# A two-layer encoder in split float32: the feed-forward part in four chunks of 3, 3, 3 and 2 column groups instead of three of 4, 4 and 3

## The chip, the cores and the metric

The kernel runs on one core of one Trainium2 chip. The metric is the device time of one execution in microseconds (us). Before the change the median of three runs is 2045.35 us (2045.31 to 2046.12). 0.2% of that is 4.1 us.

## The reference

Two layers over 256 tokens of width 2048. Each layer has a token mixer (layer 0 gates within 128-token chunks, layer 1 is grouped-query attention) and a cross-attention into 256 memory tokens, which share one input and one output projection, and then a feed-forward network (FFN) of inner width 5632. All inputs are float32. What matters here:

```python
def swiglu(h, w_gate_up, w_down):
    gate, up = jnp.split(h @ w_gate_up, 2, axis=-1)      # h: 256 x 2048, w_gate_up: 2048 x 11264
    return (jax.nn.silu(gate) * up) @ w_down             # w_down: 5632 x 2048

for l in range(2):
    ...
    x = x + jnp.concatenate([tok_out, mem_out], axis=-1) @ w_out[l]
    x = x + swiglu(rms_norm(x, g_ffn[l]), w_gate_up[l], w_down[l])
```

## The kernel before

**Split products.** Every float32 operand is split into a high half (rounded to float32r) and a low half (the rest). ScalarE makes the high half of weights (L254, `whi`), VectorE the low half (L255, `wlo`: the raw weights less `whi`). One product of 128 x 128 activations with 128 x 512 weights is three matmuls (`matmul3`, L198 to L200): high by high, low activations by high weights, high activations by low weights.

**Column groups and chunks.** The FFN has 11 column groups `f`, each 512 columns of gate and the same 512 of up. A chunk is a run of groups: first gate_up is computed for every group of the chunk, then the part of w_down that takes the chunk's features is added to the residual tiles `X`. Before the change the chunks are groups 0 to 3, 4 to 7 and 8 to 10.

**Pairs.** The class `Pair` does two 128-token rows (t = 0, 1) times two 512-column blocks at once. Its unit `i` is a pair of 128-feature rows, 2 x 2 blocks of weights: 1 MB, fetched by two DMAs into one of four `raw` tiles. A unit is done in one of two ways. `eight` does the plain eight products, 24 matmuls. `seven` does seven products in Strassen's manner, 21 matmuls; it needs four additions on the weights (L347 to L350, in `prepare`: one in place, three into a tile `T` of which there are two), one more pair of halves (of the 128 x 1536 `T`), and sums of the activations (`activation_sums`: four 128 x 128 subtractions, L303 to L306, and a split). At the end of its last `seven` unit a Pair folds the PSUM banks 1, 5, 6 and 7 together on VectorE (`inner`, L397 to L401) and adds the results into the output (L405); at the end of each half (t) of its last unit it adds the banks 2, 3, 4 and 8 (`outer`, L413). Banks 1, 5, 6 and 7 come from one ring of four PSUM tiles (`m`, which the transposes use as well), banks 2, 3, 4 and 8 from another (`acc`).

**Rings that pace the weights.** `raw` has 4 tiles, `whi` and `wlo` 3 each. A `seven` unit takes two of `whi` and two of `wlo` (raw and T), an `eight` one of each.

**A chunk's stages.** gate_up of one group is a Pair of 8 units, three of them `seven` (two in group 0). After it, ScalarE and VectorE make silu(gate) x up (L785, L786), and `turn_a` transposes the result on TensorE (L204), splits it (L192, L193) and, for units in `quick`, makes the activation sums. w_down of a chunk is two Pairs one after the other (`jj` = 0, 1, each 1024 output columns), each over all feature pairs of the chunk, two per group. `quick` names the feature pairs that are done as `seven`: in a chunk of four, two of eight; in the last chunk of three, none in layer 0 and one in layer 1. In w_down the order of a four-group Pair is, counted within the chunk, 0, 2, 1, 4, 3, 5, 6, 7 for `jj` = 0 and 1, 0, 3, 2, 4, 5, 6, 7 for `jj` = 1, with 1 and 3 as `seven`.

**What sets the order.** Small steps (`turn_a`, the additions of `inner`, the norms of the next layer) are put off by a count of ticks (`later`); each Pair unit ticks twice. The last group of a chunk is turned at the third and fourth tick of w_down, the other groups at the 12th and 13th tick of the next gate_up. The order in which the program is written is a priority: at build, a planner lays each engine's instructions into one fixed list by its own estimate of when each could run, so a list can hold the high-half products of a later unit ahead of the low-half products of an earlier one. On the chip each list runs in that order.

**The end of each layer's FFN.** In the last chunk of layer 0 each finished pair of `X` blocks starts the norm of layer 1 (`residual_turns`); in that of layer 1 the blocks are stored to the output.

Of the kernel before, what the change touches and what calls it, by code (L numbers as in the profile page):

```python
# [53 lines left out]
def encoder(ctx: ExitStack, tc: tile.TileContext, x, mem, g_mix, g_ffn, w_in_a, g_v_a, w_spatial, b_spatial,  # L54
# [16 lines left out]
    def nm(s):  # L71
        uid[0] += 1
        return f"{s}_{uid[0]}"

    def big(dt=F32, shape=None):
        return room["p"].tile(shape or [P, NB], dt, tag="a", name=nm("a"))
# [4 lines left out]
    def misc():  # L81
        return psm.tile([P, NB], F32, tag="m", name=nm("m"))

    def v4(a):
        return a.rearrange("p (c n) -> p c n", n=P)
# [10 lines left out]
    def later(delay, fn):  # L96
        queue.append((clock[0] + delay, len(queue), fn))
# [39 lines left out]
    def gslice(kind, l):  # L137
        return gcol[kind][:, 16 * l:16 * l + 16]
# [49 lines left out]
    def split(src, shape):  # L188

        hi = big(F32R, shape)  # L190
        lo = big(F32R, shape)
        nc.scalar.copy(hi, src)  # L192
        nc.vector.tensor_tensor(lo, src, hi.bitcast(F32), ALU.subtract)  # L193
        return hi, lo
# [7 lines left out]
    def transpose4(src, dst):  # L202
        for c in range(4):
            nc.tensor.transpose(dst[:, c * P:(c + 1) * P], src[:, c * P:(c + 1) * P], ident)  # L204
# [95 lines left out]
    def activation_sums(a0, a1):  # L300

        q = big(F32, [P, 4, P])
        nc.vector.tensor_tensor(q[:, 0], a1[:, 0], a1[:, 1], ALU.subtract)  # L303
        nc.vector.tensor_tensor(q[:, 2], a1[:, 0], a0[:, 0], ALU.subtract)
        nc.vector.tensor_tensor(q[:, 1], a0[:, 0], q[:, 0], ALU.subtract)
        nc.vector.tensor_tensor(q[:, 3], a0[:, 1], q[:, 1], ALU.subtract)  # L306
        hi, lo = split(q, [P, 4, P])
        return [(hi[:, i, :], lo[:, i, :]) for i in range(4)]
# [290 lines left out]
    def residual_turns(j, norm, g, parts):  # L599
        add_residual(None, j, norm, g, parts)  # L600
# [4 lines left out]
    for l in range(DEPTH):  # L605
# [151 lines left out]

        hT = Parts()
        next_norm = Norm()
        for chunk in (range(0, 4), range(4, 8), range(8, 11)):  # L760
            aT, aS, half = Parts(), {}, {}
            quick = [2 * f + 1 for f in chunk[:2 if chunk[-1] < 10 else l]]

            def turn_a(a, t, f, aT=aT, aS=aS, half=half, quick=quick):
                tp = misc()
                transpose4(a, tp)
                hi, lo = split(v4(tp), [P, 4, P])
                for i in range(4):
                    aT.put(4 * f + i, t, hi[:, i, :], lo[:, i, :])
                i = 2 * f + 1  # L770
                if i in quick:
                    half[i, t] = big(F32, [P, 2, P])
                    nc.scalar.copy(half[i, t], v4(tp)[:, 2:4])
                    if t == NT - 1:
                        aS[i] = activation_sums(half[i, 0], half[i, 1])

            pairs = {}
            for f in chunk:
                order, some = ((3, 4, 5, 0, 6, 1, 7, 2), 2) if f == 0 else ((0, 3, 1, 4, 2, 5, 6, 7), 3)
                pairs[f] = Pair(hF, sums, w_gate_up[l], f * NB, DFF + f * NB, order, fast[:some])  # L780
            for f, g in pairs.items():
                g.run(pairs.get(f + 1))
                for t in range(NT):
                    a = kp.tile([P, NB], F32, tag="sg", name=nm("sg"), bufs=2)
                    nc.scalar.activation(a, g.out[t][0], AF.Silu, scale=norm.r[t])  # L785
                    nc.vector.scalar_tensor_tensor(a, g.out[t][1], norm.r[t], a, ALU.mult, ALU.mult)  # L786
                    later(3 + t if f == chunk[-1] else 12 + t, lambda a=a, t=t, f=f: turn_a(a, t, f))
            last = chunk[-1] == 10
            every = [2 * f + c for f in chunk for c in range(2)]
            slow = [i for i in every if i not in quick]  # L790
            pairs = []
            for jj in range(2):
                order = list(slow)
                for n, i in enumerate(quick):
                    order.insert(2 * n + (0 if jj and not last else 2), i)
                into = [[X[t][2 * jj + n] for n in range(2)] for t in range(NT)]
                pairs.append(Pair(aT, aS, w_down[l], 2 * jj * NB, (2 * jj + 1) * NB, order, quick, into))
            for jj, g in enumerate(pairs):
                g.run(None if jj else pairs[1])
                for j in (2 * jj, 2 * jj + 1):  # L800
                    if last and l < DEPTH - 1:
                        residual_turns(j, next_norm, gslice("mix", l + 1), hT)
                    elif last:
                        for t in range(NT):
                            parts = 2 if j == 3 and t == NT - 1 else 1
                            for i in range(parts):
                                cs = slice(i * NB // parts, (i + 1) * NB // parts)
                                eng = nc.scalar if i else nc.sync
                                eng.dma_start(out[0, t * P:(t + 1) * P, j * NB + cs.start:j * NB + cs.stop],
                                              X[t][j][:, cs])  # L810
# [37 lines left out]
```

## Time and profile before

| | |
|---|---|
| median of 3 runs | 2045.35 us |
| profiled execution, whole | 2045.77 us |
| its span, first to last instruction | 2044.0 us |
| TensorE (PE) busy | 2028.7 us, 99% |
| VectorE (DVE) busy | 1604.7 us, 79% |
| ScalarE (ACT) busy | 1095.1 us, 54% |
| weights and others moved by DMA | 396.08 MB, 194 GB/s in the mean |

The busy times of PE are unions of instructions whose ends are modelled; how fast it really goes is read from the distance between the starts of matmuls. A busy time of VectorE counts its instructions once where two overlap. The FFN of layer 0 runs from about 340 to 1030 us of the span, that of layer 1 from about 1355 us to the end.

### The profile page before, as it was taken

What the parts mean: (1) busy time and instruction counts of PE and PEld (TensorE: products, weight loads), DVE (VectorE), ACT (ScalarE), POOL (GpSimd) and SP (SyncE); (2) the same over time, 40 slices, a digit from 0 to 9 for tenths busy, and PEclk for the clock granted to TensorE, in tenths of its full rate; (3) what the DMA queues carried; (4) which work ended last, traced back from release to release, by engine and by line L of the source; (5) the groups of instructions that cost most, each with busy time, mean ns of one, the idle gap of its engine ahead of it and who ended that gap; (6) DMA issues with size and microseconds to landing.
All of it is one profiled execution on the core that took longest, in us unless ns stands there. A gap on an engine that the chain in (4) does not pass through costs nothing.

```text
span 2044.0 us, 24691 instructions
## 1 busy us (share of the span) xinstructions
PE 2028.7 (99%) x9298; PEld 1679.5 (82%) x9298; DVE 1604.7 (79%) x1862; ACT 1095.1 (54%) x1389; POOL 49.1 (2%) x80
## 2 busy tenths in 40 slices
PE   8999999999999999999999999999999999999999
PEld 6888888888888888888888888888888888888887
DVE  5575557998888988887666876589979899798976
ACT  7765455455444554445556665555544455444552
POOL 2010000000000000000010100000000000000000
PEclk9999999999999999999999999999999999999999
DMA  9754554655656556566556434655666555665554
GB/s 330 249 177 159 187 187 148 227 168 203 208 190 220 169 201 208 200 215 209 188 190 212 157 124 142 206 179 172 205 206 211 200 176 195 206 216 196 181 197 138
DMA packets 202432, 396.08 MB, mean 194 GB/s; under 512 B 11068, under 2 KB 11432, under 8 KB 202312
## 3 DMA queue, kind: packets, MB, share of 16 engines
q1 hardware_dynamic: 198800, 385.79, 56.4%
q0 software_dynamic: 2048, 6.42, 1.0%
q10 hardware_dynamic: 1464, 2.28, 0.3%
q8 instruction: 73, 1.20, 0.2%
q14 instruction: 47, 0.39, 0.1%
HBM read 390.26 MB, written 4.19 MB: 193 GB/s over the span
## 4 chain that ended last, share of the span: by engine, by line
PE 94%; DVE 3%; DMA 1%; issue 1%; ACT 1%; SPq 0%; DVEq 0%; ACTq 0%
PE acc L200 27%; PE acc L198 27%; PE acc L199 27%; PE m L200 4%; PE m L198 4%; PE m L199 4%; PE m L204 2%; DVE wlo L255 1%; DMA raw<-in_w_gate_up 1%; ACT whi L254 0%; PE m L500 0%; DMA x<-in_x 0%; DMA raw<-in_w_down 0%; PE m L643 0%; DVE x L413 0%
## 5 line engine op out<-in xcount | busy, mean ns | idle before, releaser
L255 DVE TENSOR_TENSOR wlo<-raw,whi 128x2048 fp32r<-128x2048 f32 (+2 forms) x465 | 836.4, 1822 | 227.0 <-ACT whi L254 224.8
L254 ACT CAST whi<-raw 128x2048 fp32r<-128x2048 f32 (+2 forms) x465 | 700.9, 1539 | 584.6 <-PE acc L199 513.3
L198 PE MATMUL acc<-whi,h 128*128 128x512 f32 x1440 | 563.6, 392 | 0.8 <-ACT whi L254 0.8
L199 PE MATMUL acc<-whi,h 128*128 128x512 f32 x1440 | 562.6, 391 | 0.0
L200 PE MATMUL acc<-wlo,h 128*128 128x512 f32 x1440 | 523.8, 392 | 1.1 <-DVE wlo L255 1.1
L198 PE MATMUL acc<-whi,a 128*128 128x512 f32 x1062 | 415.4, 392 | 0.6 <-DVE a L431 0.6
L199 PE MATMUL acc<-whi,a 128*128 128x512 f32 x1062 | 414.9, 391 | 0.0
L200 PE MATMUL acc<-wlo,a 128*128 128x512 f32 x1062 | 398.8, 391 | 0.1
L200 PEld LDWEIGHTS acc<-wlo,h 128*128 128x128 f32 x1440 | 270.6, 188 | 56.9 <-DVE wlo L255 1.9
L198 PEld LDWEIGHTS acc<-whi,h 128*128 128x128 f32 x1440 | 270.7, 188 | 55.4 <-ACT whi L254 1.2
L199 PEld LDWEIGHTS acc<-whi,h 128*128 128x128 f32 x1440 | 270.6, 188 | 55.0
L200 PEld LDWEIGHTS acc<-wlo,a 128*128 128x128 f32 x1062 | 199.7, 188 | 41.5 <-DVE wlo L255 0.5
L198 PEld LDWEIGHTS acc<-whi,a 128*128 128x128 f32 x1062 | 199.9, 188 | 41.3 <-DVE a L431 0.8
L199 PEld LDWEIGHTS acc<-whi,a 128*128 128x128 f32 x1062 | 199.9, 188 | 40.5
L254 ACT CAST whi<-T 128x1536 fp32r<-128x1536 f32 x82 | 121.4, 1481 | 143.3 <-PE acc L199 104.1
L255 DVE TENSOR_TENSOR wlo<-T,whi 128x1536 fp32r<-128x1536 f32 x82 | 143.5, 1750 | 38.8 <-ACT whi L254 38.8
L198 PE MATMUL m<-whi,a 128*128 128x512 f32 x264 | 104.2, 395 | 0.7 <-ACT whi L254 0.7
L199 PE MATMUL m<-whi,a 128*128 128x512 f32 x264 | 102.8, 390 | 0.0
L347 DVE TENSOR_TENSOR raw<-raw 128x512 f32<-128x512 f32 x82 | 56.1, 684 | 56.4 <-DMA raw<-in_w_gate_up 54.3
L200 PE MATMUL m<-wlo,a 128*128 128x512 f32 x264 | 89.6, 389 | 0.0
L192 ACT CAST a<-m 128x512 fp32r<-128x512 f32 x80 | 46.3, 586 | 50.7 <-PE m L204 32.6
L193 DVE TENSOR_TENSOR a<-m,a 128x512 fp32r<-128x512 f32 x80 | 54.0, 683 | 17.5 <-ACT a L192 17.5
(126 smaller groups left out, 1469.0 us busy)
## 6 DMA issues: line engine op xcount, KB each, us to landing
raw<-in_w_gate_up SPq DMA_DIRECT2D x352, 512.0 KB, 4.7
raw<-in_w_down SPq DMA_DIRECT2D x176, 512.0 KB, 5.2
raw<-in_w_out SPq DMA_DIRECT2D x32, 1024.0 KB, 5.1
raw<-in_w_in_a SPq DMA_DIRECT2D x24, 1024.0 KB, 5.3
raw<-in_w_in_b SPq DMA_DIRECT2D x24, 1024.0 KB, 5.2
raw<-in_w_mem_kv SPq DMA_DIRECT2D x16, 1024.0 KB, 5.2
raw<-in_w_in_a SPq DMA_DIRECT2D x7, 512.0 KB, 6.1
x<-in_x SPq DMA_DIRECT2D x8, 256.0 KB, 5.7
```

The lines of the kernel that those rows point to most:

```text
L192: nc.scalar.copy(hi, src)
L193: nc.vector.tensor_tensor(lo, src, hi.bitcast(F32), ALU.subtract)
L198: nc.tensor.matmul(out, lhsT=a[0], rhs=b[0], start=start, stop=False)
L199: nc.tensor.matmul(out, lhsT=a[1], rhs=b[0], start=False, stop=False)
L200: nc.tensor.matmul(out, lhsT=a[0], rhs=b[1], start=False, stop=stop)
L204: nc.tensor.transpose(dst[:, c * P:(c + 1) * P], src[:, c * P:(c + 1) * P], ident)
L254: nc.scalar.copy(hi[:, cut], raw[:, cut])
L255: nc.vector.tensor_tensor(lo[:, cut], raw[:, cut], hi[:, cut].bitcast(F32), ALU.subtract)
L347: nc.vector.tensor_tensor(raw[:, 0], raw[:, 0], raw[:, 1], ALU.add)
```

## The change

The FFN's chunks become groups 0 to 2, 3 to 5, 6 to 8 and 9 to 10. In the first three, two of six feature pairs of w_down are `seven` units; in the last, of four feature pairs, none is, in either layer.

```diff
         hT = Parts()
         next_norm = Norm()
-        for chunk in (range(0, 4), range(4, 8), range(8, 11)):
+        for chunk in (range(0, 3), range(3, 6), range(6, 9), range(9, 11)):
             aT, aS, half = Parts(), {}, {}
-            quick = [2 * f + 1 for f in chunk[:2 if chunk[-1] < 10 else l]]
+            quick = [2 * f + 1 for f in chunk[:2 if chunk[-1] < 10 else 0]]
```

The orders of units follow from code that is not edited. In a chunk of three they are 0, 2, 1, 4, 3, 5 for `jj` = 0 and 1, 0, 3, 2, 4, 5 for `jj` = 1, with 1 and 3 as `seven`; in the chunk of two, 0, 1, 2, 3 both times. gate_up of a group is the same work as before.

## Rows read from the trace of the kernel before

**Rows 1.** The page, part 1: busy us (share of span), instructions.
```profile
PE 2028.7 (99%) x9298; PEld 1679.5 (82%) x9298; DVE 1604.7 (79%) x1862; ACT 1095.1 (54%) x1389; POOL 49.1 (2%) x80
...
PEclk9999999999999999999999999999999999999999
```

**Rows 2.** The page, part 4: the chain that ended last, by engine.
```profile
PE 94%; DVE 3%; DMA 1%; issue 1%; ACT 1%; SPq 0%; DVEq 0%; ACTq 0%
```

**Rows 3.** Waits: who waited for whom, us in total, times, longest.
```profile
ACT whi L254 <- PE acc L199: 617.4, 225, 7.4
...
DVE raw L347 <- DMA raw<-in_w_down: 2.1, 3, 1.3
```

**Rows 4.** Windows: four w_down stages of both layers, then one gate_up group.
```profile
core 0: us, PE busy (x) PEld busy (x) DVE busy (x) ACT busy (x) POOL busy (x), PEclk, DMA share, GB/s
494.69:580.47 85.78, 85.66 (x382) 70.45 (x380) 71.76 (x70) 38.06 (x25) 0.00 (x0) 1.00 0.60 196
749.31:835.15 85.84, 85.65 (x382) 70.45 (x381) 72.59 (x72) 38.07 (x25) 0.00 (x0) 1.00 0.58 196
961.48:1029.56 68.08, 68.08 (x314) 56.46 (x312) 39.86 (x43) 34.65 (x56) 2.16 (x4) 1.00 0.61 190
1508.23:1593.59 85.36, 85.36 (x381) 70.53 (x380) 71.77 (x70) 38.03 (x25) 0.00 (x0) 1.00 0.60 197
...
666.64:709.07 42.43, 42.43 (x193) 35.14 (x192) 38.56 (x41) 23.77 (x20) 0.00 (x0) 1.00 0.60 199
```

**Rows 5.** Timeline, PE in layer 0's second w_down stage: start, duration.
```profile
797.18 0.39 PE L199 MATMUL acc<-whi,a 128*128 128x512 f32 x1
...
798.77 0.39 PE L199 MATMUL acc<-whi,a 128*128 128x512 f32 x1
...
799.73 0.40 PE L199 MATMUL m<-whi,a 128*128 128x512 f32 x1
800.32 0.50 PE L198 MATMUL m<-whi,a 128*128 128x512 f32 x1 [0.19 <-ACT whi L254]
```

**Rows 6.** Groups by line and form: busy us, mean ns of one, idle before.
```profile
L255 DVE TENSOR_TENSOR wlo<-raw,whi 128x2048 fp32r<-128x2048 f32 x264 | 599.4, 2285 | 105.7 <-ACT whi L254 104.9
...
L255 DVE TENSOR_TENSOR wlo<-T,whi 128x1536 fp32r<-128x1536 f32 x82 | 143.5, 1750 | 38.8 <-ACT whi L254 38.8
...
L413 DVE TENSOR_TENSOR x<-acc,x 128x512 f32<-128x512 f32 x48 | 31.9, 684 | 12.6 <-PE acc L200 12.6
...
L304 DVE TENSOR_TENSOR a<-a,a 128x128 f32<-128x128 f32 x15 | 4.2, 282 | 0.0
```

**Rows 7.** Timeline, DVE and PEld in layer 0's first w_down stage.
```profile
517.53 1.76 DVE L255 TENSOR_TENSOR wlo<-T,whi 128x1536 fp32r<-128x1536 f32 x1 [4.07 <-ACT whi L254]
...
520.62 0.69 DVE L347 TENSOR_TENSOR raw<-raw 128x512 f32<-128x512 f32 x1 [1.34 <-DMA raw<-in_w_down]
521.24 2.28 DVE L255 TENSOR_TENSOR wlo<-raw,whi 128x2048 fp32r<-128x2048 f32 x1
...
523.57 0.19 PEld L200 LDWEIGHTS acc<-wlo,a 128*128 128x128 f32 x1 [0.54 <-DVE wlo L255]
...
541.92 1.28 DVE L413 TENSOR_TENSOR x<-acc,x 128x512 f32<-128x512 f32 x2
543.12 4.48 DVE L255 TENSOR_TENSOR wlo<-raw,whi 128x2048 fp32r<-128x2048 f32 x2
```

**Rows 8.** Timeline, the last group's turn in layer 0's last w_down stage.
```profile
969.65 0.60 PE L204 MATMUL m<-ident,sg 128*128 128x128 f32 x4
...
970.92 2.29 DVE L255 TENSOR_TENSOR wlo<-raw,whi 128x2048 fp32r<-128x2048 f32 x1 [4.52 <-ACT whi L254]
...
972.84 0.60 PE L204 MATMUL m<-ident,sg 128*128 128x128 f32 x4
...
973.13 0.68 DVE L193 TENSOR_TENSOR a<-m,a 128x512 fp32r<-128x512 f32 x1
...
977.00 0.68 DVE L193 TENSOR_TENSOR a<-m,a 128x512 fp32r<-128x512 f32 x1
```

## The prediction

> **What bounds the kernel now.** [...] The list of waits shows in which direction the pressure goes: ScalarE's high halves waited 617 us for PE to give a weight buffer back, while VectorE's wait for a w_down transfer sums to 2.1 us [rows 3]. So nearly everything runs ahead of PE up to its buffers, and the time is the number of matmuls times their distance, plus the few places where PE's list is held up. The distance: from the start at 797.18 to that at 798.77 there are seven steps, 0.227 us each [rows 5]; a four-group w_down stage holds 2 x (6 x 24 + 2 x 21) = 372 matmuls, 84.4 us at this distance, and 8 transposes, and takes 85.36 us undisturbed [rows 4]. I take the 0.227 us.
>
> The places where PE is held up: of the four four-group stages one takes 85.36 us and three take 85.78, 85.84 and 85.84 us (one row stands for the two) [rows 4]. The excess, 0.42 to 0.48 us, is one stall in each. In the first a step is 0.54 us late for a low half that VectorE finished late, since its list held an addition that waited 1.34 us for a transfer just ahead [rows 7]. In the second it is the step from 799.73 to 800.32, 0.36 us over 0.227, for a high half of T [rows 5]. Together 1.4 us. The stages where VectorE is busiest without any stall of PE are gate_up groups: 38.56 of 42.43 us, 91% [rows 4].
>
> **Removed: matmuls.** Units done as `seven` in w_down, per `jj`: before 4 in layer 0 (2 + 2 + 0) and 5 in layer 1 (2 + 2 + 1), after 6 in each. Three more, times two `jj`, times three matmuls: 18 matmuls fewer, all on PE's list, which is the path. 18 x 0.227 = 4.1 us less. Transposes stay at their number. [...] The trace shows 227 ns, and I keep that.
>
> **Added off the path.** On VectorE two adjacent 128x512 additions take 1.28 us together where one alone takes 0.68, so a follower costs 0.60; two low halves of 2048 take 4.48 where one takes 2.28, so 2.20; for T's low half of 1750 ns I take 1.67 likewise [rows 6, 7]. Six more T's: 6 x (4 x 0.60 + 1.67) = 24.4 us. Two more `inner` with their four additions: 2 x 8 x 0.60 = 9.6 us. Four more Pairs, each four `outer` additions: 9.6 us. Three more sets of activation sums, (4 x 0.28 + 0.60) each: 5 us [rows 6]. About 49 us, so VectorE goes from 79% to 81% of the span. Over the whole this is hidden under PE. ScalarE gets six more high halves of T; at 38 of 86 us in a w_down stage it has room [rows 4]. The number and size of weight transfers are unchanged; only their order on SP's queue changes, w_down's loads of a chunk standing one group earlier. No semaphore is added ahead of a transfer, and the four raw tiles pace them as before. POOL's queue is not passed by anything that moves.
>
> **Moved: less cover in a w_down stage.** This is where the gain can go. Per stage a four-group w_down has VectorE busy 71.76 of 85.78 us, 84% [rows 4]. A three-group stage loses two eights in each `jj`: four low halves, 8.8 us of VectorE, but 96 matmuls, 21.8 us of PE. What stays is 63.0 us of VectorE in 64.0 us of PE: 98%, above the 91% that is seen without a stall. And it comes in a burst. Between the last `seven` of `jj` = 0 and the first of `jj` = 1 three eights lie today, one after. From the end of that last `seven`, PE takes 5.4 us for the one eight and 4.8 us for the next `seven`. Within these 10.2 us VectorE owes `inner` (2.4 us), which frees the banks, raw's and T's low halves (2.2 + 1.7), and `outer` (2.4): 8.7 us, about 9.5 with the start behind ScalarE's copy. The four additions into X (2.4) can come later. It fits with next to nothing to spare; the next T additions (2.4) and low halves then follow in the eight after. So the stage should run about as today, with PE held up by some tenths wherever a list was laid out tighter than the chip runs. At the change from `jj` = 1 to the next gate_up three eights lie where five lie now: 16.3 us of PE against 2.4 + 2.4 + 6.6 + 2.4 + 2.4 + 3.9 = 20.1 us, the last 6 of which may run into the 4.8 us of gate_up's first `seven` and behind it; the gate_up group has 3.9 us of room [rows 4] to get this back.
>
> The price per stage a: below, 0 (as in the stage of 85.36 us). Above, VectorE keeps all the idle time that it has now at the start of a stage. Its stage has 14.0 us of idle now; 1.0 is left for it after. Of the idle time at the start 4.07 + 1.34 us [rows 7] can be filled with T additions and a low half of `jj` = 1, whose loads stand two units earlier. If another third of the 14, some 4.3 us, can't be filled, the stage is 3.3 us longer. So 0 to 3.3 us; I take 0.6, near the 0.42 to 0.48 us of the stages that stall today, a little more since the room is less. Six stages: 3.6 us, in place of today's 1.4: 2.2 us more. Nothing lets me think that it goes below today's total by more than the 1.4.
>
> **Moved: the last chunk.** Its w_down has only two units before the first that needs the last group's activations, four before. In layer 0 the transposes of that group start 8.2 and 11.4 us after the stage's start at 961.48, and the low halves are done at 973.81 and 977.68, 12.3 and 16.2 us after it; VectorE was held by a 2.29 us low half of weights in front of the first [rows 8]. After, PE comes to the first half of the third unit at 48 x 0.227 + 1.2 for the transposes = 12.1 us, and to the second at 14.8 us. In the written order its second matmul wants the low half: 0.2 and about 1.2 us late. With the eight products of a half that want only high halves put first (8 x 0.227 = 1.8 us) nothing is late. So 0 to 1.4 us a layer; I take 0.4, since PE's list does put high halves first in the stages of today [rows 5]; two layers, 0.8 us. VectorE has room there (39.86 of 68.08 us [rows 4]). Four more changes from Pair to Pair cost PE nothing of their own where VectorE is on time.
>
> **Sum.** Against the profiled execution, 2045.77 us with 1.8 us outside its span: -4.1 + 2.2 + 0.8 = -1.1 us. It lies 0.4 us above the median of the runs; applied to the median, 2045.35 - 1.1 = 2044.3 us.
>
> **Rivals.** (A) VectorE becomes the bound in the three-group w_down stages. Place: from the end of the last `seven` of `jj` = 0 on. It decides from where the 8.7 us above don't get into 10.2 us, for instance because a T addition that waits for its transfer stands ahead of them in VectorE's list, as at 520.62 [rows 7]. At 2.0 us a stage (the middle of the upper half of 0 to 3.3, rounded down): -4.1 - 1.4 + 12 + 0.8 = +7.3, 2052.7 us; at 3.3, 2060.5. For it: the 98%, and that 1.34 us of such a wait made PE 0.54 us late already. Against: PE's list takes high-half products first, so a late low half costs less than its lateness. [...]
> (B) The full saving: the lists come out as well as in the stage of 85.36 us, and today's stalls go as well. 2045.35 - 4.1 = 2041.3 us, and with the 1.4 us 2039.9. For it: three stages of four stall only by one step. Against: less room in every one.
> (C) The last chunk's turn is in the way, 1.4 us in each layer and as much again because the fourth unit waits too: -4.1 + 2.2 + 5.6 = +3.7, 2049.0 us. Against: VectorE's room there.
> (D) The matmuls are not saved, since the count of `seven` units doesn't rise: excluded by the counts above, unless PE is not the path; 2% for that.
>
> **Chances.** Forecast (2042 to 2048) 0.50, A 0.27, B 0.14, C 0.07, D 0.02. This kernel can be told from no change by about 0.2%, 4.1 us. Faster by more needs 2041.2 or less: most of B, 0.13. Slower by more is 2049.5 or above: A nearly whole and a third of C, 0.28. Within: 0.59. The range for 8 in 10: it leaves out the faster half of B and the longer half of A: 2041 to 2053 us.
>
> **What would show it.** Right: 9280 matmuls on PE in place of 9298; start-to-start distances of 0.227 us still; three-group w_down stages of about 64 to 65 us, with VectorE at 95% or more of them; stalls of tenths at low halves near the change of `jj`; last stages with the turn's halves just in time. Wrong, for A: steps of over 1 us on PE that end with VectorE's low halves, with `inner` (a PSUM bank) or with `outer`, in each of six stages. For C: one step over 1 us in each last stage, released by L193. The forecast is wrong too if the stages are as predicted and the time is lost elsewhere, in the mixer of layer 1 for instance, whose lists are laid out anew.

## The result and the profile after

The changed kernel takes 2055.82 us (median of five, 2053.64 to 2056.99) where the kernel before takes 2045.52 us (five, 2045.31 to 2046.52): a ratio of 1.0049, 95% interval 1.0038 to 1.0059, 10 us slower. The forecast was 2044.3 us, the range ended at 2053. The profiled execution took 2055.82 us with a span of 2054.0 us, 10.0 us more than before.

The page after, parts 1 and 4 (busy us, share of the span, instructions; the chain that ended last):

```profile
PE 2030.6 (99%) x9280; PEld 1676.9 (82%) x9280; DVE 1651.4 (80%) x1939; ACT 1104.4 (54%) x1406; POOL 48.6 (2%) x80
...
PE 93%; DVE 4%; ACT 1%; DMA 1%; issue 1%; SPq 0%; DVEq 0%; ACTq 0%
```

The 18 matmuls are gone [rows 1], VectorE has 47 us more to do, and nothing on the page looks like a loss: PE is still busy 99%. The loss shows in the steps between the starts of matmuls. Beyond the 0.227 us that each step takes anyway, the long steps (0.33 us and more) of the FFN, from each layer's first w_down stage on, sum to 15.5 us after and 1.3 us before. Almost two thirds of that is one event that comes six times, at the end of each three-group chunk: a step of 1.743 or 1.744 us and a lengthened one behind it, together 1.63 us more than two steps of 0.227.

Windows of the changed kernel: the w_down stages of the first two chunks, the gate_up group behind the second, and the last w_down stage of layer 0 (columns as in [rows 4]):

```profile
451.77:515.84 64.07, 63.88 (x285) 52.44 (x284) 60.45 (x65) 31.02 (x22) 0.00 (x0) 1.00 0.61 196
644.24:708.79 64.55, 64.17 (x286) 52.36 (x284) 60.47 (x65) 31.08 (x23) 0.00 (x0) 1.00 0.59 195
708.79:751.30 42.51, 41.15 (x182) 33.76 (x181) 37.34 (x36) 20.10 (x13) 0.00 (x0) 1.00 0.59 196
986.86:1033.41 46.55, 46.55 (x218) 38.37 (x216) 30.64 (x39) 27.19 (x52) 0.00 (x0) 1.00 0.56 181
```

The w_down stages themselves are nearly what was forecast: 64.07 to 64.61 us with VectorE at 94% (forecast 64 to 65 us, 95% or more), and the last stage is held up by only 0.24 us. The lost time lies behind the stage, in the first microseconds of the next gate_up. The timeline of PE there, in the first chunk of layer 0 (start, duration, and in brackets the idle time and what ended it):

```profile
515.84 0.39 PE L198 MATMUL m<-whi,h 128*128 128x512 f32 x1
...
520.60 0.39 PE L199 MATMUL acc<-whi,h 128*128 128x512 f32 x1
522.34 0.50 PE L198 MATMUL m<-whi,h 128*128 128x512 f32 x1 [1.35 <-ACT whi L254]
```

gate_up begins at 515.84. Behind the matmul of 520.60 the next one in PE's list is the first of the next seven, and it waits for that unit's high half. ScalarE began that half at 520.39, when PE had given a `whi` tile back:

```profile
520.39 1.90 ACT L254 CAST whi<-raw 128x2048 fp32r<-128x2048 f32 x1 [2.62 <-PE acc L199]
```

No matmul starts between 520.60 and 522.34, 0.05 us after the end of this half (522.29): this one late half holds PE. The products of the eight that stand behind it in the list had things to come from VectorE: the eight's low half, and the last banks that `outer` has to free. Its timeline in the same stretch:

```profile
513.71 1.75 DVE L255 TENSOR_TENSOR wlo<-T,whi 128x1536 fp32r<-128x1536 f32 x1
515.37 0.69 DVE L348 TENSOR_TENSOR T<-raw 128x512 f32<-128x512 f32 x1
515.98 0.69 DVE L413 TENSOR_TENSOR x<-acc,x 128x512 f32<-128x512 f32 x1
516.58 1.29 DVE L405 TENSOR_TENSOR x<-x,e 128x512 f32<-128x512 f32 x2
517.78 0.69 DVE L413 TENSOR_TENSOR x<-acc,x 128x512 f32<-128x512 f32 x1
518.38 0.69 DVE L347 TENSOR_TENSOR raw<-raw 128x512 f32<-128x512 f32 x1
518.98 0.69 DVE L349 TENSOR_TENSOR T<-T,raw 128x512 f32<-128x512 f32 x1
519.58 0.69 DVE L350 TENSOR_TENSOR T<-T,raw 128x512 f32<-128x512 f32 x1
520.18 2.29 DVE L255 TENSOR_TENSOR wlo<-raw,whi 128x2048 fp32r<-128x2048 f32 x1
522.38 1.29 DVE L413 TENSOR_TENSOR x<-acc,x 128x512 f32<-128x512 f32 x2
```

There is no bracket in it: VectorE never waits. The low half is done at 522.5, the last two `outer` additions at 523.7, 7.8 us after PE left w_down. In the kernel before the same place, PE's change to gate_up at 580.47, looks like this:

```profile
580.38 0.68 DVE L413 TENSOR_TENSOR x<-acc,x 128x512 f32<-128x512 f32 x1
580.99 0.68 DVE L348 TENSOR_TENSOR T<-raw 128x512 f32<-128x512 f32 x1
581.58 0.68 DVE L413 TENSOR_TENSOR x<-acc,x 128x512 f32<-128x512 f32 x1
```

All banks are free 1.8 us after the change, and no step there is long.

### The profile page after: what moved, and what is told of

It is laid out like the page before. It is cut to its first block, busy times and chain, and to the rows that moved or that the text cites. A ratio compares the mean times of both kernels' runs of the same rounds, so it can differ in the third digit from the quotient of the medians.

```text
span 2054.0 us, 24742 instructions
## 1 busy us (share of the span) xinstructions
PE 2030.6 (99%) x9280; PEld 1676.9 (82%) x9280; DVE 1651.4 (80%) x1939; ACT 1104.4 (54%) x1406; POOL 48.6 (2%) x80
## 3 DMA queue, kind: packets, MB, share of 16 engines
q0 software_dynamic: 2048, 6.42, 1.0%
## 4 chain that ended last, share of the span: by engine, by line
PE 93%; DVE 4%; ACT 1%; DMA 1%; issue 1%; SPq 0%; DVEq 0%; ACTq 0%
PE acc L200 26%; PE acc L198 26%; PE acc L199 26%; PE m L200 4%; PE m L198 4%; PE m L199 4%; PE m L204 2%; DVE wlo L255 2%; ACT whi L254 1%; DMA raw<-in_w_gate_up 1%; PE m L500 0%; DVE x L413 0%; PE m L643 0%; DMA x<-in_x 0%; DVE e L413 0%
## 5 line engine op out<-in xcount | busy, mean ns | idle before, releaser
L198 PE MATMUL acc<-whi,a 128*128 128x512 f32 x1032 | 402.7, 393 | 1.5 <-ACT whi L254 0.9
L199 PE MATMUL acc<-whi,a 128*128 128x512 f32 x1032 | 402.8, 391 | 0.0
L200 PE MATMUL acc<-wlo,a 128*128 128x512 f32 x1032 | 385.2, 392 | 1.0 <-DVE wlo L255 1.0
L254 ACT CAST whi<-T 128x1536 fp32r<-128x1536 f32 x88 | 130.4, 1482 | 193.3 <-PE acc L199 162.9
L198 PEld LDWEIGHTS acc<-whi,a 128*128 128x128 f32 x1032 | 194.1, 188 | 43.6 <-ACT whi L254 3.5
L200 PEld LDWEIGHTS acc<-wlo,a 128*128 128x128 f32 x1032 | 194.1, 188 | 42.8 <-DVE wlo L255 3.0
L199 PEld LDWEIGHTS acc<-whi,a 128*128 128x128 f32 x1032 | 194.3, 188 | 39.7 <-DVE a L193 0.8
L255 DVE TENSOR_TENSOR wlo<-T,whi 128x1536 fp32r<-128x1536 f32 x88 | 154.5, 1755 | 27.3 <-ACT whi L254 26.6
L198 PE MATMUL m<-whi,a 128*128 128x512 f32 x288 | 112.9, 392 | 0.4 <-ACT whi L254 0.4
L199 PE MATMUL m<-whi,a 128*128 128x512 f32 x288 | 112.1, 389 | 0.0
L347 DVE TENSOR_TENSOR raw<-raw 128x512 f32<-128x512 f32 x88 | 60.4, 687 | 55.5 <-DMA raw<-in_w_gate_up 55.4
L200 PE MATMUL m<-wlo,a 128*128 128x512 f32 x288 | 98.8, 389 | 0.0
```

The costliest lines, as they stand in the source:

```text
L198: nc.tensor.matmul(out, lhsT=a[0], rhs=b[0], start=start, stop=False)
L199: nc.tensor.matmul(out, lhsT=a[1], rhs=b[0], start=False, stop=False)
L200: nc.tensor.matmul(out, lhsT=a[0], rhs=b[1], start=False, stop=stop)
L254: nc.scalar.copy(hi[:, cut], raw[:, cut])
L255: nc.vector.tensor_tensor(lo[:, cut], raw[:, cut], hi[:, cut].bitcast(F32), ALU.subtract)
L347: nc.vector.tensor_tensor(raw[:, 0], raw[:, 0], raw[:, 1], ALU.add)
```

## The experiments

Three theories were put up. V: VectorE's sum over a three-group w_down stage is too near PE's (as rival A had it). B: the boundary from w_down to gate_up costs 1.6 us by the order in PE's list, whatever VectorE has to do. W, formed after the first eight runs: what counts is the burst that VectorE owes between the last seven of `jj` = 1 and the first seven of gate_up. All times are medians with the range of the runs, beside runs of the kernel before on the same chip; that one had medians of 2045.7 to 2045.9 us there, single runs from 2043.8 to 2048.1.

**No seven in w_down.**

```diff
-            quick = [2 * f + 1 for f in chunk[:2 if chunk[-1] < 10 else 0]]
+            quick = [2 * f + 1 for f in chunk[:0]]
```

> The changed kernel with every w_down unit as eight products (chunks of 3, 3, 3 and 2 alone): 72 matmuls more than the changed kernel, 54 more than the kernel before, 12.2 us at 0.227. Theory V (VectorE is the bound in the three-group w_down stages, and PE is held up for it): without T's and inner's VectorE has about 40 of 66 us to do, PE is held up nowhere in w_down, so 2045.5 + 12.2 - 1.4 (today's stalls) + 0.5 = 2056.8 us, within 1. Rival B (the boundary from w_down to gate_up costs 1.6 us by itself, through the order in PE's list, each time a chunk of three ends): six of them stay, 9.8 us more, 2066 us.

2056.74 us (2056.52 to 2057.79), as V had it: four chunks cost nothing by themselves, and the boundary has no stall of its own.

**One seven instead of two.**

```diff
-            quick = [2 * f + 1 for f in chunk[:2 if chunk[-1] < 10 else 0]]
+            quick = [2 * f + 1 for f in chunk[:1 if chunk[-1] < 10 else 0]]
```

> The changed kernel with one seven-product unit instead of two in each w_down Pair of the first three chunks: 36 matmuls more than the changed kernel, 18 more than before, +4.1 us. Theory V: VectorE has some 55 of 65.5 us to do in a stage, 84%, as in the four-group stages of before; stalls 0 to 0.45 us a stage, so 2048.2 to 2051 us, faster than the changed kernel in spite of 36 matmuls more. Rival B: the 1.6 us at each w_down end stays, 2058 to 2060 us, slower than the changed kernel.

2048.42 us (2046.29 to 2051.28): 36 matmuls more than the changed kernel, and 7 us faster. B is out as a cost of every boundary, whatever VectorE has to do.

**Without the additions of inner into X.**

```diff
             if o:
                 for (t, n), x, op in (((0, 0), e, ALU.add), ((0, 1), f, ALU.add), ((1, 0), v, ALU.subtract),
                                       ((1, 1), y, ALU.add)):
-                    later(1 + 2 * t + n, lambda o=o[t][n], x=x, op=op: nc.vector.tensor_tensor(o, o, x, op))
+                    pass
```

> The changed kernel without the four additions of inner into X (L405; left out, so the inner banks' sums don't reach the output): 2.4 us less on VectorE in each Pair, 4.8 us in each stage, the same matmuls. Theory V: a stage has 58 of 64 us of VectorE, 91%, the share at which gate_up groups show no stall; most of the 14 us of stalls goes, 2042 to 2046 us. Rival B (PE's list, the ring of three high halves): the same lists of matmuls and the same rings, 2054 to 2056 us.

2044.43 us (2042.76 to 2045.08), ratio to before 0.9994 (0.9985 to 1.0003). Taking 2.4 us off VectorE in each Pair gives 11 us back; the six steps of 1.74 us are gone. The step at the change of `jj` (0.58 us, a high half of ScalarE's) stays.

**More work on VectorE in the kernel before**, first without, then with a tie to the unit's weights.

```diff
+                if self.into and len(self.order) == 8:
+                    for _ in range(3 if n % 4 == 1 else 2):
+                        nc.vector.tensor_tensor(junk, junk, junk, ALU.max)
                 (self.seven if i in self.fast else self.eight)(i, *self.ready.pop(i))
```

> The kernel before with 2 or 3 maxima on a 128x256 tile of its own on VectorE per unit of the four-group w_down stages (36 a stage, about 12 us), which changes no value that is read: VectorE 84 of 85.8 us, 98%, as in the three-group stages of the changed kernel. Theory V: the load alone makes the stalls, 1 to 4 us in each of four stages, 2049 to 2061 us. Rival B: stages of four have three eights after the last seven, and no chunk boundary changes, so at most 1 us more, 2045 to 2046.5 us.

2057.7 us (2055.98 to 2058.43), but this tells nothing of w_down: nothing tied the maxima to their place, and the planner laid the first of them out at 328 us, ahead of the FFN. Long steps stand in the first gate_up group (3.02 us at 368.7). With `w = self.ready[i][0][:, 0, :2 * P]` read in place of `junk`:

> As the run with more work on VectorE, but each maximum reads the unit's raw weights, so that it can't be laid out before they have landed: 36 maxima of 128x256 in each of the four four-group w_down stages (about 12 us a stage, 98% of it). Theory V: the load makes the stalls where it stands, 1 to 4 us in each of four stages, 2049 to 2061 us, the stalls between 494 and 590 us and at the like places, none in the first gate_up groups. Rival B: the four-group stage with its three eights takes it, 2045 to 2047 us.

2051.87 us (2051.05 to 2052.68), ratio 1.0028 (1.0017 to 1.004). The four-group stage, too, stalls under the load alone, as V said and B did not; VectorE's groups between 494 and 582 us show the load, PE's timeline where it bites (the banks that `outer`, here L417, frees at the change of `jj`):

```profile
L338 DVE TENSOR_TENSOR junk<-raw 128x256 f32<-128x256 f32 x30 | 12.5, 418 | 1.1 <-DMA raw<-in_w_down 0.8
```

```profile
545.51 0.50 PE L198 MATMUL acc<-whi,a 128*128 128x512 f32 x1 [0.71 <-DVE x L417]
```

PE is held up by 1.3 to 2.4 us a stage, early and in the middle of it. VectorE was busy 93 to 95% of these stages, not the 98% that was meant, since only 30 or 31 of the 36 maxima lie in each; that is about the 94% of the changed kernel's stages. At the end, behind five eights, PE's change to gate_up has no long step.

**An eight first in gate_up.**

```diff
                 order, some = ((3, 4, 5, 0, 6, 1, 7, 2), 2) if f == 0 else ((0, 3, 1, 4, 2, 5, 6, 7), 3)
+                if f == chunk[0] and f:
+                    order = (3, 0, 4, 1, 5, 2, 6, 7)
```

> The changed kernel with the first gate_up group of the second to fourth chunk in the order 3, 0, 4, 1, 5, 2, 6, 7 instead of 0, 3, 1, 4, 2, 5, 6, 7, so that an eight follows w_down and T is wanted 5.4 us later. Rival B (the stall of 1.6 us comes from the order in which the lists meet there): the six stalls go, 2045 to 2047 us. Theory V: VectorE is as late as before, and an eight wants the banks of outer at once where a seven wants them 2.7 us later, so the stall stays or grows, 2053 to 2062 us.

2045.3 us (2043.25 to 2048.24), ratio to before 0.9997 (0.9987 to 1.0006). V expected the stall to stay; it is gone, as B had it here, with the same matmuls and the same work on VectorE. B, as a cost whatever VectorE has to do, is out by the runs above, and so is V as it stood: it is not the sum over the stage that decides. VectorE's `outer` at the same place:

```profile
518.36 0.68 DVE L413 TENSOR_TENSOR x<-acc,x 128x512 f32<-128x512 f32 x1
...
519.56 1.28 DVE L413 TENSOR_TENSOR x<-acc,x 128x512 f32<-128x512 f32 x2
```

The banks are free at 520.8, 4.3 us after PE's change to gate_up at 516.49 instead of 7.8, as T's low half has moved behind them.

**The additions left out in one half only** (`if o and self.na:` leaves them out in `jj` = 0, `if o and not self.na:` in `jj` = 1).

> The changed kernel with inner's four additions into X left out in the first w_down Pair of each stage (jj = 0) alone; its inner banks' sums don't reach the output. Theory W (the stalls come from what VectorE owes in a burst between the last seven of jj = 1 and the first seven of gate_up): the six stalls of 1.6 us stay, only those at the change of jj can shrink, 2052 to 2056 us. Theory V (the sum over the stage, 98%): 2.4 us less a stage, whichever half, takes about half of the 11 us that the run without all the additions gained, 2049 to 2051 us.

> The same additions left out in the second w_down Pair (jj = 1) alone. Theory W: the six stalls go, 9.8 us, 2045 to 2047 us. Theory V: as with those of the first Pair, 2049 to 2051 us.

2054.16 us (2052.36 to 2055.0) without those of `jj` = 0, 2046.97 us (2045.53 to 2047.7) without those of `jj` = 1: W in both. The first run still has the step of 1.74 us in all six places; PE in the first chunk:

```profile
521.20 0.39 PE L199 MATMUL acc<-whi,h 128*128 128x512 f32 x1
522.94 0.50 PE L198 MATMUL m<-whi,h 128*128 128x512 f32 x1 [1.36 <-ACT whi L254]
```

and VectorE's last `outer` at 524.3; in the second run it is done at 517.7, and no long step is left there:

```profile
515.79 0.68 DVE L413 TENSOR_TENSOR x<-acc,x 128x512 f32<-128x512 f32 x1
...
517.00 0.68 DVE L413 TENSOR_TENSOR x<-acc,x 128x512 f32<-128x512 f32 x1
```

The same 2.4 us are worth 1.7 us in the first Pair, within the spread of the runs, and 9 us in the second.

One thing these two runs do not separate. The planner lays PE's list out anew for every kernel, and where the stall is gone the list is another one. In the changed kernel, and without the additions of `jj` = 0, 22 matmuls stand between the start of gate_up and the next seven's first one, in all six places. Without those of `jj` = 1, as without any, it is 29: more products of the eight come first, and when PE reaches the next seven its high half is there:

```profile
515.67 0.39 PE L198 MATMUL m<-whi,h 128*128 128x512 f32 x1
...
522.24 0.39 PE L198 MATMUL m<-whi,h 128*128 128x512 f32 x1
```

In the changed kernel the chain of the stall runs from PE to ScalarE and back to PE; in the first 10 us of these six gate_up groups no row of PE waits for VectorE. With the list as it is, the step would stand even if VectorE had been earlier. So the runs show that the work owed there decides, but it acts through the list. That the planner drew the next seven forward because VectorE was late in its own estimate too is argued, not shown: no run kept the list and changed VectorE's work at that place.

**Trying to win: the additions on GpSimd**, in the changed kernel (`nc.gpsimd` for `nc.vector` in that line), and in chunks of 4, 4 and 3 with two sevens in every chunk (`chunk[:2]`). In the latter some of the last Pair's additions come behind the store of its block, so the output lacks them.

> The changed kernel with inner's four additions into X (L405) on GpSimd instead of VectorE. Theory V: VectorE has 58 of 64 us to do, as in the run without these additions, 2043 to 2047 us, if an addition on GpSimd is done in some 2 us and does not slow VectorE; no run here has shown either yet. Rival B: 2054 to 2056 us as the changed kernel.

> The kernel before, chunks of 4, 4 and 3, with two seven-product units in the last chunk of both layers (the same 18 matmuls fewer as in the changed kernel) and inner's additions into X on GpSimd. Theory V: 4.1 us less, the four-group stages with 62 of 85.8 us of VectorE and two three-group stages instead of six at 91%: 2040.5 to 2044 us, faster than both kernels, if GpSimd costs VectorE nothing. If GpSimd's additions slow VectorE or come late: 2045 us or more.

2064.25 us (2064.06 to 2065.17) and 2061.33 us (2060.24 to 2064.0), both a miss. In the first, by groups:

```profile
L255 DVE TENSOR_TENSOR wlo<-T,whi 128x1536 fp32r<-128x1536 f32 x88 | 160.6, 1825 | 28.9 <-ACT whi L254 28.8
...
L405 POOL TENSOR_TENSOR x<-x,e 128x512 f32<-128x512 f32 x48 | 83.5, 1755 | 1065.9 <-DVE x L413 954.5 <-DVE e L400 44.8 <-DVE e L399 41.3
```

An addition takes 1.76 us instead of 0.68, T's low half in the mean 1825 ns instead of 1755. What costs is not a wait for GpSimd: none of VectorE's idle time in this run ends with one of its additions. PE, ScalarE and VectorE have the same lists here, row by row in line and tile, as in the run without the additions, which took 2044.43 us; so the 19.8 us between the two come from the additions themselves. Rows of VectorE that read no PSUM bank grow, 36 us in all against the median of the like rows: in the mean the last T addition (L350) takes 830 ns where the changed kernel has 688, the addition in place (L347) 732 instead of 687, the low half of 2048 2326 instead of 2287. One of them beside GpSimd:

```profile
485.53 1.60 POOL L405 TENSOR_TENSOR x<-x,e 128x512 f32<-128x512 f32 x1 [154.26 <-DVE x L413]
...
485.90 1.78 DVE L350 TENSOR_TENSOR T<-T,raw 128x512 f32<-128x512 f32 x1
```

The last T addition took 1.78 us beside GpSimd in each of 12 cases, 0.68 elsewhere; `outer`, which reads a PSUM bank, kept its 0.68 us (679 ns in the mean of its 64 rows). PE pays where `outer` or a low half comes late behind such rows (for instance 0.94 us at 488.33, released by L413). In the run of 4, 4 and 3 one such wait took 3.55 us (to 1000.57, released by L413).

**Trying to win: an eight first in the second w_down Pair as well**, and then, in the kernel before, the eight first in gate_up alone.

```diff
-                    order.insert(2 * n + (0 if jj and not last else 2), i)
+                    order.insert(2 * n + (1 if jj and not last else 2), i)
```

> The run with an eight first in gate_up, and also an eight first in the second w_down Pair: its order 0, 1, 2, 3, 4, 5 instead of 1, 0, 3, 2, 4, 5. Theory W: the stalls at the change of jj (4.6 us in all) go too, since T is wanted 5.4 us later there, 2040.5 to 2043 us, faster than the kernel before. Against it: only two eights are left behind the last seven of the stage, so the burst before gate_up comes back, 0.5 to 1.6 us in each of six, 2044 to 2051 us.

2051.53 us (2050.19 to 2052.57): the counter-argument held. With two eights behind the last seven of the stage instead of three, PE waits for `outer` twice behind each stage:

```profile
517.91 0.19 PEld L198 LDWEIGHTS acc<-whi,h 128*128 128x128 f32 x1 [0.49 <-DVE x L413]
523.78 0.19 PEld L198 LDWEIGHTS acc<-whi,h 128*128 128x128 f32 x1 [0.55 <-DVE x L413]
```

and the stall at the change of `jj` did not go; it became a wait for a low half of VectorE's (0.54 us from start to start, to 485.67).

> The kernel before with an eight first in the first gate_up group of the second and third chunk. By W and V alike: there is no stall at that place before, with five eights behind the last seven, so nothing to win, 2044.5 to 2046.5 us. If it gains over 2 us, the order itself is worth something that no stall shows.

2044.73 us (2043.99 to 2045.97), ratio 0.9996 (0.9986 to 1.0005): nothing, as there was no stall to remove. No version tried is faster than the kernel before by more than the measurement can tell.

## Why the prediction was wrong

**Right.** The term of the matmuls: 9280, steps of 0.227 us, -4.1 us. The stages: 64.07 to 64.61 us, VectorE 94%, just under the 95% or more that was given. At the change of `jj`, priced with the rest at 0.6 us a stage: the changed kernel has ten long steps there or just behind, 4.6 us in six stages, 0.8 each. The last chunk: 0.24 us a layer instead of 0.4. With the 1.3 us of long steps before, that is so far -4.1 + 4.6 - 1.3 + 0.5 = -0.3 us, near the forecast's -1.1.

**The step that failed.** "At the change from `jj` = 1 to the next gate_up three eights lie where five lie now: 16.3 us of PE against [...] 20.1 us, the last 6 of which may run into the 4.8 us of gate_up's first `seven` and behind it; the gate_up group has 3.9 us of room [...] to get this back." The sum of 20.1 us was worked out and then given no price, on the ground that it could be made up later. But room in a later 42 us does not help a wait that falls due in the first five: the first seven and the eight behind it need T's halves and all four `acc` banks, and VectorE had both behind each other in one list. In the lists that came of it, 1.63 us was lost in each of six places, 9.8 us: with -0.3 and some 0.7 us of small steps that makes about the 10.0 us measured. The forecast also had no term for what such a burst does to PE's list: the next seven stood 22 matmuls behind the boundary, too early for its high half. The excess of that very sum over PE, 20.1 - 16.3 = 3.8 us, named the place, and the 1.63 us lies within it; the price of 0 to 3.3 us a stage was drawn from the stage's total instead, and taken near the stalls of today, which stand in stages with five eights at the end.

**The rivals.** A had, in VectorE, the engine whose work decides and, with 2052.7 us, nearly the size. It had the wrong place (the change of `jj`), and its sign, steps over 1 us that end with a low half, `inner` or `outer`, is not what the rows show: all six end with ScalarE's high half. Its ground, 98% over the stage (94% measured), is not what decides: with the same work an eight put first takes the stall away, and 2.4 us less in the first Pair hardly shortens the time. What A held against VectorE's list, that work for later stands ahead of what PE needs, shows at the place found too: PE's last w_down matmul began at 515.61, but the last `outer` (522.38) stands behind T additions and a low half, none of them waiting.

**What stays open.** Why the step is 1.743 or 1.744 us in all six places is read from the trace (ScalarE's 1.90 us behind the release of a `whi` tile), but whether a fourth `whi` and `wlo` tile alone would hide it was not tried. Whether VectorE's burst would hold PE on the chip if the list of the run without the additions of `jj` = 1 met the changed kernel's load was not tried either.

## What to carry to other kernels

Where a helper engine is near its limit, don't stop at its share of a stage: list what it owes between two fixed points of the bound engine, here from the last unit that creates work to the first that needs the buffers back, and price the excess there, even if the next stage has room. Shorter stages move those points together. When such a burst is found, the order of units at the boundary can be a cheaper lever than the amount of work: here one line of order was worth 10 us, a change of 18 matmuls 4. It cuts both ways, since another line of order cost 6 us. And read the bound engine's list at that place before and after: a planner that estimates times lays it out anew with every change.

## What the runs showed of the hardware

In the run of 4, 4 and 3 with GpSimd, one step of PE took 3.94 us (996.63 to 1000.57), and the next three took 0.32, 0.43 and 0.43 us, not 0.227 (starts at 1000.89, 1001.32 and 1001.75). The granted clock of that stretch, and of the next:

```profile
1000.50:1004.00 3.50, 3.43 (x9) 2.73 (x10) 3.50 (x5) 1.85 (x7) 2.54 (x2) 0.55 0.91 280
1004.50:1010.00 5.50, 5.50 (x29) 4.55 (x28) 5.11 (x7) 1.09 (x5) 2.99 (x2) 1.00 0.61 200
```

0.55 is the mean over the first window, 1.00 that over the second. PE starts nine matmuls in the 3.43 us from 1000.57 to the first window's end; nine steps of 0.227 are 2.04. So at least 1.4 us came on top of the wait. Behind the six waits of 1.74 us in the changed kernel the granted clock is 1.00, and after one step of 0.34 us the steps are 0.225 to 0.236 us. What lowered the clock in the one stretch no run shows.
